# A decay mask added by one VectorE instruction per chunk, and the per-token column moved into the bias of eight ScalarE exponentials

## The chip, the cores and the metric

The kernel runs on one core of one Trainium2 chip. The metric is device time in microseconds of one execution. Five engines matter here: TensorE (PE, with its weight loads shown apart as PEld), VectorE (DVE), ScalarE (ACT), GpSimd (POOL) and SyncE (SP), which issues the DMAs. Each engine works through its own instruction queue in order and waits on semaphores of the others.

## The reference, cut to what matters

The program is one layer of a hybrid backbone, run over 128 context tokens and 1024 noisy tokens with the same weights. Its parts are an adaLN modulation, an input projection, a bidirectional chunked scan (SSD) beside a chunk MLP, an output projection, and a squared-ReLU channel MLP. The change lies in the scan, which works in 9 chunks of 128 tokens with 16 heads in 4 groups, once in each direction:

```
a_cum = jnp.cumsum(dtc * A.reshape(G, hg), axis=2)
xdt = xc * dtc[..., None]
seg = a_cum[:, :, :, None] - a_cum[:, :, None, :]
decay = jnp.exp(jnp.where(mask, seg, -jnp.inf))
cb = jnp.einsum('bcign,bcjgn->bcijg', Cc, Bc)
y_diag = jnp.einsum('bcijgh,bcjghp->bcighp', cb[..., None] * decay, xdt)
```

For each chunk, head and direction there is thus a 128x128 matrix exp(row value of token i - column value of token j), masked to one triangle. The kernel folds ln(dt) of token j into the column value, so that the matrix already carries the factor dt.

## The kernel before, in words

Features lie on partitions, tokens on the free axis, in three slices of 384 tokens. Products in full precision are three passes of rounded high and low parts (`product`, L182). A weight tile is split into these parts by `split` (L167): ScalarE makes the high part, and GpSimd or VectorE makes the low part by a subtraction (L169).

The input projection is a stream of 32 column tiles (L549 to L554): for each of the 4 groups B, C and two x tiles and some u tiles, then eight z tiles. The order of TensorE's work is written out by hand: `product` calls `tick` three times on the way, and `tick` runs a piece of a generator: a convolution pass (`conv`, L607), transposes, or a piece of `scan` (L680). The other engines' queues are ordered by a planner that goes by its own costs and by the order of the program.

`scan(g, G)` first walks the chunks backward to build the states of the backward direction (L742 to L756), then forward over all nine chunks (L760 to L795). Per chunk the forward loop updates the state `Hf` (TensorE into the one bank `Sps`, VectorE L765), builds the matrices of the chunk three further on with `mats` (L710), multiplies into the one bank `yp` (L785), and ScalarE copies that bank out (L788).

`mats(c)` is called 36 times, 9 per group. It loads `ap`, 128 partitions (token j) by 8 x 128 (4 heads of either direction, token i), broadcast from DRAM. For c > 0 ScalarE writes `ea = exp(ap)` (L717) and GpSimd multiplies it by C (L718). Then VectorE runs eight instructions on 128x128 each (L720), which add to `ap` the column value `lcol` of token j as a per-partition scalar and the mask of the direction; ScalarE takes two exponentials of 128x512 (L723); VectorE adds the two directions into `M` (L725), and GpSimd multiplies by C B (L726).

Of the kernel before, what the change touches and what calls it, by code (L numbers as in the profile page):

```python
# [10 lines left out]
AF = mybir.ActivationFunctionType  # L11
# [3 lines left out]
P = 128  # L15
# [15 lines left out]
# columns of the table of per-feature vectors, features on partitions  # L31
# [33 lines left out]
def cut(c0, c1):  # L65
    """Columns c0:c1 by the sequence they belong to: (start, stop, v)."""
    if c0 < TP < c1:
        return [(c0, TP, 0), (TP, c1, 1)]
    return [(c0, c1, int(c0 >= TP))]
# [10 lines left out]
def cc(c):  # L80
    """Columns of chunk c in a convolved tile, which keeps a gap of 4 behind the prompt."""
    return slice(c * P + 4, c * P + 4 + P) if c else slice(0, P)
# [3 lines left out]
def hybrid_layer(ctx, tc, i, y_out, st_out):  # L86
# [14 lines left out]
    def phase(**sizes):  # L101
        # a phase's pools; each tile waits only for the last users of its own bytes
        nonlocal stack
        stack.close()
        stack = ExitStack()
        for nm in list(pools):
            if nm not in ("x1", "sq"):
                del pools[nm]
        for nm, n in sizes.items():
            pools[nm] = stack.enter_context(tc.tile_pool(name=nm, bufs=n, reuse_waits="tile"))  # L110
# [19 lines left out]
    # ---- scratch in DRAM  # L130
# [9 lines left out]
    # ---- constants  # L140
# [30 lines left out]
    def wtile(src, name, tag="w", lo_eng=None):  # L171
        """A weight tile of 1024 words per partition as its high and low part."""
        if tag == "w":
            raw = wp.tile([P, KD, P], F32, tag="raw", name=name + "r", bufs=2)
            hi, lo = (wp.tile([P, KD, P], F32R, tag="w", name=name + x, bufs=4) for x in "hl")
        else:
            raw = tl(tag + "r", name + "r", (KD, P))
            hi, lo = (tl(tag, name + x, (KD, P), F32R) for x in "hl")
        nc.sync.dma_start(raw, src)
        split(hi, lo, raw, lo_eng or nc.gpsimd)  # L180
        return hi, lo

    def product(ps, w, act, beside=None):
        """ps = W.T @ act over the 8 k-tiles, in three passes of rounded parts; beside() runs three times on the way."""
        wh, wl = w
        ah, al = act
        n = 0
        for k in range(KD):
            for a, b in ((wh, ah), (wh, al), (wl, ah)):
                nc.tensor.matmul(ps, a[:, k, :], b[:, k, :], start=n == 0, stop=n == 3 * KD - 1)  # L190
                n += 1
                if beside and n % KD == 0:
                    beside()

    def rms_factor(reds, name):
        """1/sqrt(mean of squares + eps) of the columns, on all partitions; reds: squares that add up over the features."""
        w = reds[0].shape[-1]
        ps = mps(name + "p", w)
        for n, r in enumerate(reds):
            nc.tensor.matmul(ps, ones, r, start=n == 0, stop=n == len(reds) - 1)  # L200
        rs = med(name + "s", (w,))
        nc.scalar.activation(rs, ps, AF.Sqrt, bias=eps_t, scale=1.0 / D)
        nc.vector.reciprocal(rs, rs)
        return rs

    def modulate(xk, s, gain, sh0, hs, rs, ks=range(KD)):
        """h = x * rs * gain + shift for token slice s, as high and low part."""
        c0 = s * SL
        for a, b, v in parts(s):
            r = slice(a - c0, b - c0)  # L210
            for k in ks:
                o = med("hn")[:, :b - a]
                nc.vector.scalar_tensor_tensor(out=o, in0=xk[k][:, r], scalar=gain[:, k, v:v + 1], in1=rs[:, r],
                                               op0=ALU.mult, op1=ALU.mult)
                nc.scalar.activation(hs[0][:, k, r], o, AF.Identity, bias=modT[:, sh0 + k, v:v + 1])
                nc.vector.scalar_tensor_tensor(out=hs[1][:, k, r], in0=o, scalar=modT[:, sh0 + k, v:v + 1],
                                               in1=hs[0][:, k, r].bitcast(F32), op0=ALU.add, op1=ALU.subtract)

    # ======== conditioning, positions, first norm
# [18 lines left out]
    def first_ada(q):  # L238
        """Shift and gain of two feature tiles of the first norm, in steps of two k-tiles."""
# [26 lines left out]
    def ada(r):  # L266
        """A third of the modulation vectors, in steps of one k-tile."""
# [29 lines left out]
    def place(x, k, s, eng):  # L297
        """x = feature tile k of token slice s with its positions."""
# [11 lines left out]
    def square(x, acc):  # L310
        """acc + x * x; acc None starts the sum."""
        sq = med("sq")
        nc.scalar.activation(sq, x, AF.Square)
        if acc is not None:
            nc.vector.tensor_tensor(out=sq, in0=sq, in1=acc, op=ALU.add)
        return sq

    def first_norm(s):
        """The rows of token slice s, feature tile by feature tile, and their rms factor."""
# [44 lines left out]
    # ======== dt and v, tokens on partitions; chunk MLP over tokens  # L364
# [3 lines left out]
    # small pieces of work for the tensor engine, run between parts of the products: generators that yield the  # L368
    # least distance to their next piece
# [25 lines left out]
    def v_products(n, k, js, pss, s):  # L395
        """Adds feature tile k to the products of the token chunks js with a third of the columns of dt and v."""
# [11 lines left out]
    # the first products run feature tile by feature tile beside the vectors that their rows need  # L408
# [53 lines left out]
    def mix(s, vgs):  # L462
        """Layer norm of v and its products with the chunk's mixing weights."""
# [28 lines left out]
    def decay_rates():  # L492
        """Softplus, decays; columns: group, direction, head of the group."""
# [13 lines left out]
        # dt  # L507
        nc.vector.scalar_tensor_tensor(out=t0, in0=A, scalar=0.0, in1=t2, op0=ALU.max, op1=ALU.add)
        # ln dt: the argument of a tiny softplus is its logarithm
# [3 lines left out]
        # dt * A, cumulated from either end  # L513
# [35 lines left out]
    # ---- the products of the input projection: kind, number within the kind, column tile  # L549
# [34 lines left out]
    # the first product of the input projection fills the tensor engine while the last mix is under way  # L584
# [8 lines left out]
    # ======== the rest of the input projection; the scan runs beside it  # L593
    phase(xtm=1, mask=1, st=6, M=3, xw=1, xs=6, hf=2, yo=2, cb=1, H=2, B=2, cv=4, xp=2, m=2)
    # added to the exponents: 0 on and below the diagonal, above it for the other direction
# [6 lines left out]
    # ---- pieces of the scan of a group  # L602
# [4 lines left out]
    def conv(kind, g, m, xp):  # L607
        """Convolution, bias and silu of a tile of channels, one pass at a time; then what the scan needs of it."""
# [23 lines left out]
    def totm(src, put, gap):  # L632
        """Transposes of the chunks of src[128 channels, tokens], four at a time."""
# [46 lines left out]
    def scan(g, G):  # L680
        """The scan of group g; yields after pieces of work on the tensor engine."""
# [5 lines left out]
        # states before the sample's chunks: Hb[c] backward, all kept; forward, rolling  # L687
# [18 lines left out]
        def decay(d, c, a, b):  # L706
            """b = the part of the state behind chunk c of direction d that comes from a, the one before it."""
            nc.gpsimd.tensor_tensor(out=heads(b), in0=heads(a), in1=wcol(atot, c, d), op=ALU.mult)

        def mats(c):  # L710
            """The moving operands of chunk c: decayed C B and, per direction, C times the decay from the chunk's edge."""
# [3 lines left out]
            if c:  # L715
                ea = tl("st", "ea", (8, P))
                nc.scalar.activation(ea, ap, AF.Exp)  # L717
                nc.gpsimd.tensor_tensor(out=ea, in0=ea, in1=G.CT[:, cc(c)].unsqueeze(1).to_broadcast([P, 8, P]), op=ALU.mult)  # L718
            for e in range(8):
                nc.vector.scalar_tensor_tensor(out=ap[:, e, :], in0=ap[:, e, :], scalar=lcol[:, c, 8 * g + e:8 * g + e + 1],  # L720
                                               in1=mask[:, e // 4, :], op0=ALU.add, op1=ALU.add)
            for d in (0, 4):
                nc.scalar.activation(ap[:, d:d + 4, :], ap[:, d:d + 4, :], AF.Exp)  # L723
# [74 lines left out]
    # ---- the products  # L798
# [56 lines left out]
    # ======== output projection onto the residual  # L855
# [45 lines left out]
    # chunk-MLP half of the rows  # L901
# [17 lines left out]
    # scan half, then the second norm of a token slice beside the products of the next  # L919
# [26 lines left out]
    # ======== channel MLP  # L946
# [32 lines left out]
    # feature tiles that get their gain before the rms factor is known  # L979
# [47 lines left out]
    # the last two blocks by token slice  # L1027
# [7 lines left out]
def _positions():  # L1035
    """The 2-D position table: features on rows, first by grid row, then by grid column."""
# [11 lines left out]
def _layout(x):  # L1048
# [5 lines left out]
    def wcols(w, cols):  # L1054
        """[tile, partition, k, column] of a weight matrix of 1024 rows."""
# [3 lines left out]
    def gde(a):  # L1059
        """(direction, head) to (group, direction, head of the group) on the last axis."""  # L1060
# [51 lines left out]
```

## Time and profile before

| quantity | value |
|---|---|
| device time, median of 3 runs | 1842.14 us (1841.31 to 1844.1) |
| profiled execution, from its first to its last instruction (span) | 1835.2 us |
| median of the runs less that span | 6.9 us |
| PE busy | 1721.4 us (94%) |
| PEld busy | 1651.2 us (90%) |
| DVE busy | 1105.3 us (60%) |
| ACT busy | 626.4 us (34%) |
| POOL busy | 670.3 us (37%) |

The profile is of one execution, told by its span; the time of the three runs holds some microseconds around it. Busy time of an engine is the time in which an instruction of its is under way, also where that instruction is held up after its start. A row of idle time names what ended it, inferred from semaphores. The share of busy time over the whole span mixes stages with different limits, so the stretch of the scan (about 170 us to 760 us) is read apart.

### The profile page before, as it was taken

To read this page: it belongs to the slowest core of one execution; us is meant where nothing else is said; L and a number is where in the kernel's file an instruction comes from. 1 tells how busy PE (TensorE), PEld (TensorE's weight loads), DVE (VectorE), ACT (ScalarE), POOL (GpSimd) and SP (SyncE) were. 2 spreads that over 40 slices of the span, in tenths; PEclk is the share of its full clock that TensorE was granted. 3 is DMA by queue.
4 is the path that set the end of the run, shared out by engine and by line. 5 is a ranking of instruction groups with operands and counts; after the bars stand their busy time and mean duration, and the time that the engine had idled before them with its cause. 6 is when DMAs were issued, how large, how long until landed. Compare 5 with 4: busy or idle time off the path is not lost.

```text
span 1835.2 us, 26485 instructions
## 1 busy us (share of the span) xinstructions
PE 1721.4 (94%) x10349; PEld 1651.2 (90%) x10349; DVE 1105.3 (60%) x1803; ACT 626.4 (34%) x1045; POOL 670.3 (37%) x493
## 2 busy tenths in 40 slices
PE   6999997897897898899999999999999999999996
PEld 3888997797797787899999999999999999999996
DVE  5956569969969979767388533333333334334427
ACT  4533344454444443354235311122222211111132
POOL 2300225535426426436455422223333222222244
PEclk9999999899898998999999999999999999999999
DMA  9676332242242254685243111111111111111102
GB/s 346 209 245 213 97 135 91 93 145 91 70 152 78 94 204 148 214 297 173 94 127 104 58 46 36 36 45 47 47 46 47 35 35 47 47 35 46 35 12 104
DMA packets 84925, 193.82 MB, mean 106 GB/s; under 512 B 7584, under 2 KB 47552, under 8 KB 84800
## 3 DMA queue, kind: packets, MB, share of 16 engines
q1 hardware_dynamic: 84800, 192.12, 31.5%
q8 instruction: 82, 1.34, 0.3%
q14 instruction: 43, 0.35, 0.1%
HBM read 157.27 MB, written 34.82 MB: 105 GB/s over the span
## 4 chain that ended last, share of the span: by engine, by line
PE 61%; DVE 17%; issue 5%; POOL 2%; ACT 2%; DMA 2%; SPq 0%; DVEq 0%; ACTq 0%; POOLq 0%
PE fps L190 22%; PE gps L970 20%; PE ips L190 10%; DVE ap L720 7%; PE ops L190 6%; DVE cv L613 2%; PE yp L785 1%; DVE xwl L169 1%; DVE x L988 1%; DMA ld<-yz_d 1%; DVE M L725 1%; DVE yt L842 1%; DVE red L930 1%; PE tmp L638 1%; DVE x L868 1%
## 5 line engine op out<-in xcount | busy, mean ns | idle before, releaser
L868 DVE SCALAR_TENSOR_TENSOR x<-gps,modT,x 128x128 f32<-128x128 f32 (+2 forms) x480 | 232.6, 513 | 122.6 <-PE gps L970 122.6
L961 DVE TENSOR_TENSOR fl<-r,fh 128x384 fp32r<-128x384 f32 x96 | 54.1, 565 | 363.4 <-POOL r L960 363.4
L970 PE MATMUL gps<-fh,w2h 128*128 128x384 f32 (+2 forms) x768 | 257.6, 335 | 1.5 <-DVE x L868 1.5
L970 PE MATMUL gps<-fh,w2l 128*128 128x384 f32 (+2 forms) x768 | 256.9, 334 | 0.0
L970 PE MATMUL gps<-fl,w2h 128*128 128x384 f32 (+2 forms) x768 | 256.8, 334 | 0.0
L169 POOL TENSOR_TENSOR w2l<-w2r,w2h 128x1024 fp32r<-128x1024 f32 x31 | 74.6, 2407 | 324.2 <-ACT w2h L168 324.2
L720 DVE SCALAR_TENSOR_TENSOR ap<-ap,lcol,mask 128x128 f32<-128x128 f32 x288 | 178.7, 676 | 5.3 <-ACT ea L717 2.8
L168 ACT CAST w2h<-w2r 128x1024 fp32r<-128x1024 f32 x32 | 33.6, 1051 | 339.9 <-PE gps L970 314.2
L970 PEld LDWEIGHTS gps<-fh,w2h 128*128 128x128 f32 x768 | 144.2, 188 | 2.9 <-DVE x L868 2.1
L970 PEld LDWEIGHTS gps<-fl,w2h 128*128 128x128 f32 x768 | 144.2, 188 | 0.8 <-issue 0.2
L970 PEld LDWEIGHTS gps<-fh,w2l 128*128 128x128 f32 x768 | 144.2, 188 | 0.6
L960 POOL TENSOR_TENSOR r<-r 128x384 f32<-128x384 f32 x96 | 79.7, 831 | 148.7 <-ACT fh L959 148.7
L613 DVE SCALAR_TENSOR_TENSOR cv<-xp,cw,cv 128x1156 f32<-128x1156 f32 x64 | 103.5, 1617 | 28.2 <-ACT cv L610 27.2
L169 POOL TENSOR_TENSOR wil<-wir,wih 128x1024 fp32r<-128x1024 f32 x25 | 60.1, 2404 | 164.3 <-ACT wih L168 160.1
L169 POOL TENSOR_TENSOR wol<-wor,woh 128x1024 fp32r<-128x1024 f32 x32 | 81.4, 2549 | 66.6 <-ACT woh L168 66.5
L958 ACT ACTIVATE r<-fps 128x384 f32<-128x384 f32 x96 | 46.9, 489 | 171.7 <-PE fps L190 170.7
L169 POOL TENSOR_TENSOR w1l<-w1r,w1h 128x1024 fp32r<-128x1024 f32 x32 | 77.0, 2405 | 66.5 <-ACT w1h L168 66.5
L718 POOL TENSOR_TENSOR ea<-ea,cv 128x1024 f32<-128x1024 f32 x32 | 83.9, 2621 | 21.6 <-ACT ea L717 21.1
L190 PE MATMUL ips<-h1h,wih 128*128 128x384 f32 x256 | 90.4, 353 | 0.0
L190 PE MATMUL ips<-h0h,wil 128*128 128x384 f32 x256 | 90.3, 353 | 0.0
L190 PE MATMUL ips<-h0l,wih 128*128 128x384 f32 x256 | 90.3, 353 | 0.0
L190 PE MATMUL ips<-h0h,wih 128*128 128x384 f32 x256 | 90.2, 352 | 0.0
(292 smaller groups left out, 4826.3 us busy)
## 6 DMA issues: line engine op xcount, KB each, us to landing
wa<-in_w_ada_dram SPq DMA_DIRECT2D x48, 512.0 KB, 5.4
wor<-in_w_out_dram SPq DMA_DIRECT2D x40, 512.0 KB, 3.6
ap<-arow_d SPq DMA_DIRECT2D x36, 512.0 KB, 4.1
wir<-in_w_in_dram SPq DMA_DIRECT2D x32, 512.0 KB, 3.8
w1r<-in_w_ff_dram SPq DMA_DIRECT2D x32, 512.0 KB, 3.5
w2r<-in_w_ff_dram SPq DMA_DIRECT2D x32, 512.0 KB, 3.5
mix_d<-vg SPq DMA_DIRECT2D x9, 512.0 KB, 5.1
mxt<-mix_d SPq DMA_DIRECT2D x8, 576.0 KB, 4.7
```

The source lines that it names most:

```text
L168: nc.scalar.copy(hi, src)
L169: lo_eng.tensor_tensor(out=lo, in0=src, in1=hi.bitcast(F32), op=ALU.subtract)
L190: nc.tensor.matmul(ps, a[:, k, :], b[:, k, :], start=n == 0, stop=n == 3 * KD - 1)
L613: nc.vector.scalar_tensor_tensor(out=acc, in0=xp[:, k:k + 1156], scalar=cw[:, 16 * k + m:16 * k + m + 1], in1=acc, op0=ALU.mult, op1=ALU.add)
L638: nc.tensor.transpose(ps[:, c, :], src[:, cc(c0 + c)], ident)
L718: nc.gpsimd.tensor_tensor(out=ea, in0=ea, in1=G.CT[:, cc(c)].unsqueeze(1).to_broadcast([P, 8, P]), op=ALU.mult)
L720: nc.vector.scalar_tensor_tensor(out=ap[:, e, :], in0=ap[:, e, :], scalar=lcol[:, c, 8 * g + e:8 * g + e + 1], in1=mask[:, e // 4, :], op0 ...
L868: nc.vector.scalar_tensor_tensor(out=x1[m][:, a:b], in0=ps[:, a - cols.start:b - cols.start], scalar=modT[:, g0 + m, v:v + 1], in1=x1[m][: ...
L958: nc.scalar.activation(r, ps, AF.Relu)
L960: nc.gpsimd.tensor_tensor(out=r, in0=r, in1=r, op=ALU.mult)
L961: nc.vector.tensor_tensor(out=fl[:, cs], in0=r, in1=fh[:, cs].bitcast(F32), op=ALU.subtract)
L970: nc.tensor.matmul(ps, a[:, m, :], x[:, cols], start=n == 0, stop=n == n1)
```

## The change

`mats` keeps its load, `ea` and the two products on GpSimd. One VectorE addition of 128x1024 now adds the mask to `ap`, the mask tile being read four times per direction by a broadcast view. The column `lcol` is no longer added by VectorE: it goes as bias into the exponential, and since it differs by head and direction, there are now eight exponentials of 128x128 in place of two of 128x512. Everything else in the diff is removed comments.

```diff
         def mats(c):
...
                 nc.scalar.activation(ea, ap, AF.Exp)
                 nc.gpsimd.tensor_tensor(out=ea, in0=ea, in1=G.CT[:, cc(c)].unsqueeze(1).to_broadcast([P, 8, P]), op=ALU.mult)
+            nc.vector.tensor_tensor(out=ap.rearrange("p (d e) i -> p d e i", d=2), in0=ap.rearrange("p (d e) i -> p d e i", d=2),
+                                    in1=mask.unsqueeze(2).to_broadcast([P, 2, 4, P]), op=ALU.add)
             for e in range(8):
-                nc.vector.scalar_tensor_tensor(out=ap[:, e, :], in0=ap[:, e, :], scalar=lcol[:, c, 8 * g + e:8 * g + e + 1],
-                                               in1=mask[:, e // 4, :], op0=ALU.add, op1=ALU.add)
-            for d in (0, 4):
-                nc.scalar.activation(ap[:, d:d + 4, :], ap[:, d:d + 4, :], AF.Exp)
+                nc.scalar.activation(ap[:, e, :], ap[:, e, :], AF.Exp, bias=lcol[:, c, 8 * g + e:8 * g + e + 1])
             M = tl("M", "M", (4, P))
             nc.vector.tensor_tensor(out=M, in0=ap[:, 0:4], in1=ap[:, 4:8], op=ALU.add)
```

## Rows read from the trace of the kernel before

**Rows 1.** The page's first part: engine, busy us (share of span), instructions.
```profile
PE 1721.4 (94%) x10349; PEld 1651.2 (90%) x10349; DVE 1105.3 (60%) x1803; ACT 626.4 (34%) x1045; POOL 670.3 (37%) x493
```

**Rows 2.** The page's fourth part: shares of the last-ending chain by line.
```profile
PE fps L190 22%; PE gps L970 20%; PE ips L190 10%; DVE ap L720 7%; PE ops L190 6%; DVE cv L613 2%; PE yp L785 1%; DVE xwl L169 1%; DVE x L988 1%; DMA ld<-yz_d 1%; DVE M L725 1%; DVE yt L842 1%; DVE red L930 1%; PE tmp L638 1%; DVE x L868 1%
```

**Rows 3.** Busy us (instructions) by stretch; last PE clock, DMA share, GB/s.
```profile
core 0: us, PE busy (x) PEld busy (x) DVE busy (x) ACT busy (x) POOL busy (x), PEclk, DMA share, GB/s
280.00:360.00 80.00, 64.98 (x433) 59.20 (x433) 79.06 (x108) 32.42 (x56) 46.24 (x34) 0.87 0.23 73
400.00:500.00 100.00, 81.05 (x549) 73.80 (x548) 92.69 (x138) 50.51 (x82) 54.13 (x46) 0.91 0.30 95
540.00:640.00 100.00, 79.61 (x543) 72.44 (x542) 95.80 (x136) 45.81 (x77) 56.51 (x44) 0.91 0.29 95
680.00:760.00 80.00, 63.55 (x430) 58.60 (x430) 77.71 (x124) 31.73 (x59) 48.34 (x33) 0.89 0.43 143
sum 360.00, PE 289.19 PEld 264.05 DVE 345.26 ACT 160.47 POOL 205.21; mean PE 72.30 PEld 66.01 DVE 86.32 ACT 40.12 POOL 51.30
```

**Rows 4.** Waits in 170:760: engine, line, waited for: us, times, longest us.
```profile
ACT ap L723 <- DVE ap L720: 123.6, 52, 7.7
...
PE Sps L704 <- DVE Hf L765: 34.2, 15, 4.6
...
PE Sps L704 <- DVE H L751: 18.4, 12, 2.7
PE yp L785 <- ACT yt L788: 16.8, 11, 4.5
```

**Rows 5.** Timeline of DVE, 471.5 to 479.2: start us, us, instruction, count.
```profile
472.86 5.99 DVE L720 SCALAR_TENSOR_TENSOR ap<-ap,lcol,mask 128x128 f32<-128x128 f32 x5
478.77 0.41 DVE L765 TENSOR_TENSOR Hf<-Hf,Sps 128x256 f32<-128x256 f32 x1
```

**Rows 6.** Timeline of POOL, 471.5 to 479.2.
```profile
472.61 0.80 POOL L708 TENSOR_TENSOR H<-H,atot 128x256 f32<-128x256 f32 x1
473.37 2.46 POOL L718 TENSOR_TENSOR ea<-ea,cv 128x1024 f32<-128x1024 f32 x1
475.79 2.39 POOL L169 TENSOR_TENSOR wil<-wir,wih 128x1024 fp32r<-128x1024 f32 x1
```

**Rows 7.** Tile ap: ns min/median/max of one instruction, first and last start us.
```profile
L720 DVE SCALAR_TENSOR_TENSOR ap<-ap,lcol,mask x288: 334/340/2593, 181.7 to 752.2; 128x128 f32<-128x128 f32 x144
L723 ACT ACTIVATE ap<-ap x72: 614/630/634, 182.9 to 752.5; 128x512 f32<-128x512 f32 x72
L725 DVE TENSOR_TENSOR M<-ap x36: 674/680/2557, 184.9 to 753.2; 128x512 f32<-128x512 f32 x36
```

**Rows 8.** Timelines of DVE: five masks alone; a 128x1024 subtraction and its follower.
```profile
569.95 1.39 DVE L720 SCALAR_TENSOR_TENSOR ap<-ap,lcol,mask 128x128 f32<-128x128 f32 x5
...
714.04 1.21 DVE L169 TENSOR_TENSOR wil<-wir,wih 128x1024 fp32r<-128x1024 f32 x1
715.18 0.54 DVE L841 SCALAR_TENSOR_TENSOR th<-th,ips 128x384 f32<-128x384 f32 x1
```

**Rows 9.** Busy time of L720 alone in the four stretches.
```profile
280.00:360.00 80.00, 43.77 (x60) 0.87 0.23 73
400.00:500.00 100.00, 44.69 (x72) 0.91 0.30 95
540.00:640.00 100.00, 50.32 (x72) 0.91 0.29 95
680.00:760.00 80.00, 26.93 (x61) 0.89 0.43 143
```

**Rows 10.** ACT by line and form: busy us, mean ns | idle before it.
```profile
L215 ACT ACTIVATE h1h<-hn,modT 128x384 fp32r<-128x384 f32 x8 | 4.5, 615 | 1.5 <-DVE hn L213 1.5
...
L215 ACT ACTIVATE h0h<-hn,modT 128x128 fp32r<-128x128 f32 x8 | 2.9, 397 | 7.9 <-DVE hn L213 7.9
```

**Rows 11.** Timeline of ACT: three instructions with a bias from SBUF, and two masks' exponentials.
```profile
68.30 1.68 ACT L215 ACTIVATE h1h<-hn,modT 128x384 fp32r<-128x384 f32 x3 [1.50 <-DVE hn L213]
...
555.38 0.63 ACT L723 ACTIVATE ap<-ap 128x512 f32<-128x512 f32 x1
555.92 1.04 ACT L717 ACTIVATE ea<-ap 128x1024 f32<-128x1024 f32 x1
```

## The prediction

> **What bounds the kernel now.** I read the page first. TensorE is busy 1721.4 of 1835.2 us [rows 1], so over the whole span it looks like the bound and the change, which touches VectorE and ScalarE, like a trifle. But the chain that ended last has one line that isn't TensorE and weighs more than the rest of its kind: the masks on VectorE, L720, with 7% of the span, some 128 us [rows 2]. So the place of the change is on the path, and its stage must be read alone.
>
> I cut the scan into stretches. In four of them (one per group, 360 us together) VectorE is busy 345.26 us and TensorE only 289.19 [rows 3]: here VectorE's queue is hardly ever empty, and TensorE idles 360 - 289.19 = 70.8 us. Its clock is granted at 0.87 to 0.91 in them, so part of the stretch runs at the lower of two levels, 1.2 in place of 2.4 GHz; at 0.87 that part is 0.26 of the stretch, and TensorE fills there time in which it would otherwise wait. The waits say what TensorE stands for: 34.2 us for the state sum L765 and 18.4 us for L751, both short VectorE instructions [rows 4]. They are late because of what is queued ahead of them, and one place shows it: five masks take 5.99 us, and L765 comes right behind [rows 5].
>
> Five masks need not take that long. Where nothing disturbs them five take 1.39 us [rows 8]. Beside the 5.99 us GpSimd runs three instructions back to back, from 472.61 to 478.18 [rows 6]; 5.6 us of these and 5 x 0.26 = 1.3 us of masks make 6.9, less than 1 us over the 5.99. So VectorE and GpSimd take turns there: a mask, which reads two operands in SBUF, stands while a GpSimd instruction is under way. In the four stretches the two engines together are the bound, and that is the reading on which my number rests.
>
> **The change part by part.** *VectorE loses* eight masks per chunk. Undisturbed one lasts 0.34 us [rows 7], and they follow each other every (1.39 - 0.34) / 4 = 0.2625 us [rows 8]; eight hold the engine for 2.10 us. *It gains* one addition of 128x1024 with two operands in SBUF. The trace has the same form as a subtraction of a weight tile: 1.21 us, with the next instruction 1.14 us after its start [rows 8]. The mask's broadcast view isn't in that row, so I bound it: down to 1.14, up to the eight it replaces, 2.10, if the view were read slowly. I take 1.14, since the form and operand type are those of the row. Saved per chunk: 2.10 - 1.14 = 0.96 us.
>
> How many chunks pay? In the four stretches lie 60 + 72 + 72 + 61 = 265 of 288 masks [rows 9], that is 33.1 of 36 chunks; the rest runs where TensorE is the bound and gives nothing. The sum: 33.1 x 0.96 = 31.8 us.
>
> *The time masks were held up* is 43.77 + 44.69 + 50.32 + 26.93 = 165.7 us of busy time [rows 9] less 265 x 0.2625 = 69.6, so 96 us. I cost it at nothing: what GpSimd does is unchanged, and as long as VectorE's queue is never empty, the time that one instruction no longer stands is stood by the next. The other end is that it goes with the instructions, for one start per chunk in place of eight; that is the first rival.
>
> The Trainium skill bears on this choice (SBUF — State Buffer, section "Who interferes with whom"): a VectorE instruction with two SBUF inputs and a GpSimd instruction that reads SBUF exclude each other, and the second to issue stands until the first ends. The trace agrees at the place of [rows 5, 6]. By this rule the turns cost what both engines execute, whatever number of instructions it is cut into, and the sum stays at 31.8 us; by the masks' mean busy time in the four stretches, 165.7 / 265 = 0.63 us each, it would be 33.1 x (8 x 0.63 - 1.21), over 120 us and more than all of TensorE's idle time there.
>
> *ScalarE loses* two exponentials of 128x512 per chunk, 0.63 us each and 0.54 us apart [rows 7, 11]: 1.17 us. *It gains* eight of 128x128 with a bias from SBUF. The trace has that form: 0.397 us [rows 10]. One of 128x384 takes 0.615 us [rows 10] and three together 1.68 [rows 11], so each begins (3 x 0.615 - 1.68) / 2 = 0.08 us before its predecessor's end; an estimate from that is 0.40 + 7 x 0.32 = 2.6 us for eight. ScalarE gets 2.6 - 1.17 = 1.43 us more per chunk, 47 us over 33.1 chunks. In the four stretches it is busy 160.5 of 360 us [rows 3], afterwards about 208, still 58%; and for 123.6 us it stood waiting for masks [rows 4], which come sooner now. That cover hides the 47 us. Without it they lie in front of the copy L788, which frees the one bank `yp`: see the third rival.
>
> *The addition M* (L725) now waits for an exponential that ends about 2.6 us after the mask, not 0.63. Queued behind it on VectorE are state sums for which TensorE waits. What hides this is other VectorE work between mask and M: passes of the convolution, weighing, the next chunk's mask. The matrices are built three chunks ahead of their use, so their own lateness costs nothing. I take nothing for it; bounds: zero, and (2.6 - 0.63) x 33.1 = 65 us.
>
> No DMA, no queue of SP and no instruction of GpSimd is added or moved. What is late next in the four stretches: still GpSimd and VectorE in turn, since TensorE keeps 70.8 - 31.8 = 39 us of idle time there.
>
> **The sum.** The span 1835.2 less 31.8 is 1803.4 us. The median of the runs, 1842.14, is 6.9 us above this span, for what lies around it and from run to run; with that, 1810.3 us. I predict 1810 us, with 1800 to 1823 as this case's own range: its upper end lets a fifth of the bound of M's wait be paid (13 us), its lower end lets a tenth of the 96 us of hold-ups go after all (10 us).
>
> **The rivals.**
> *First: the hold-ups go with the instructions.* One start per chunk meets GpSimd once. Half of the 96 us goes, VectorE's queue runs empty at times, and TensorE's waits for the two state sums vanish: 34.2 + 18.4 = 52.6 us [rows 4], up to the whole 70.8. Time: 1842 - 57 = 1785, from 1771 to 1795. For it: single masks were stretched to 2.59 us [rows 7], and the first of them is released by the same exponential `ea` as GpSimd's product. Against it: VectorE is busy 96% of the four stretches, so something else stands next.
>
> *Second: M's wait eats it.* If M stands right behind the mask in VectorE's queue in half of the chunks, 33 of 65 us come back: 1842 - 32 + 33 = 1843, no change that shows.
>
> *Third, slower: ScalarE is late for TensorE.* In place: the copy L788 out of the only `yp` bank, for which TensorE already waits 16.8 us [rows 4]. If the copy stands behind the eight exponentials, the next chunk's product starts 1.43 us later, 51 us over 36 chunks: 1842 - 32 + 51 = 1861. It decides once more than six tenths of the chunks (31.8 of 51) pay. For it: one bank, one in-order queue. Against it: ScalarE's long waits for the masks, which shrink.
>
> *Fourth: it doesn't do what it says.* The addition with its broadcast mask takes 2.10 us like the eight masks; VectorE wins nothing, ScalarE's 47 us stay hidden: 1842.
>
> **How the numbers follow.** My case 0.48, the first rival 0.27, the second 0.10, the third 0.10, the fourth 0.05. A measurement of this kernel tells a change of about 0.2% (3.7 us) from none. The first two cases are faster by more: 0.75; of the second and fourth rival half, 0.05 to the faster side if they eat a little less than all, which makes 0.80; 0.08 within; 0.12 slower, from the third rival and a little of the second. The range 1775 to 1842 leaves out the lower end of the first rival (0.05) and the slower cases (0.13).
>
> **What would show it right or wrong.** Right: L720 shows 36 additions with a minimum near 1.2 us and some of 2 to 4; VectorE's busy time falls by far more than 32 us only if its queue runs empty; L723 shows 288 exponentials near 0.39 us; TensorE's idle time between 280 and 730 us falls by about 32 us, with its waits for L765 and L751 shrunken; nothing outside the scan changes. Wrong by the first rival: VectorE below 90% busy in these stretches and TensorE's idle time nearly gone. By the second: idle time of VectorE before M, ended by L723. By the third: TensorE's wait for L788 grown from 16.8 us to over 40. By the fourth: the shortest addition at 2 us.

## The result and the profile after

The changed kernel took 1808.22 us (median of 4 runs, 1807.15 to 1808.8) beside 1841.72 us for the kernel before: a ratio of 0.9822, interval 0.9808 to 0.9836, or 33.5 us less. The profiled execution has a span of 1805.4 us, 29.8 less than before; the medians and the spans come from different executions, so the two differences need not agree. All of the 29.8 us comes from the scan: from 170 us to the last copy out of `yp` it takes 565 us in place of 595, and from there to the end both kernels take 1070 us.

The page of the changed kernel begins so; it answers to [rows 1, 2]:

```profile
PE 1711.6 (95%) x10349; PEld 1644.1 (91%) x10349; DVE 1068.3 (59%) x1551; ACT 669.7 (37%) x1261; POOL 704.3 (39%) x493
...
PE fps L190 22%; PE gps L969 21%; PE ops L190 7%; PE ips L190 7%; DVE ap L719 3%; DVE cv L613 2%; ACT ap L722 2%; DVE xwl L169 1%; DVE xw L696 1%; DVE M L724 1%; DVE x L987 1%; PE yp L784 1%; DVE red L929 1%; DVE h20l L216 1%; DVE x L867 0%
```

The masks' line on the last-ending chain has gone from 7% to 3%, and the exponentials have come in with 2%. GpSimd, whose instructions are the same, is busy 34 us longer; the place shown at the end of this section says why. (Line numbers behind `mats` are one lower now.)

The tile `ap` in the changed kernel (ns min/median/max, first and last start), against [rows 7]:

```profile
L722 ACT ACTIVATE ap<-ap,lcol x288: 384/388/415, 183.1 to 724.0; 128x128 f32<-128x128 f32 x144
...
L719 DVE TENSOR_TENSOR ap<-ap,mask x36: 1210/2154/3426, 181.8 to 719.9; 128x1024 f32<-128x1024 f32 x36
L724 DVE TENSOR_TENSOR M<-ap x36: 676/688/2570, 187.3 to 724.4; 128x512 f32<-128x512 f32 x36
```

The addition's shortest instance, 1.21 us, is the row it was taken from [rows 8], so the broadcast view of the mask costs nothing. Its median is 2.15 us: most of the 36 additions are held up. The exponentials take 0.388 us.

The four stretches of the changed kernel (they lie elsewhere now), against [rows 3], and below them the waits from 170 to 740 us, against [rows 4]:

```profile
core 0: us, PE busy (x) PEld busy (x) DVE busy (x) ACT busy (x) POOL busy (x), PEclk, DMA share, GB/s
280.00:360.00 80.00, 66.80 (x486) 61.47 (x485) 76.35 (x61) 49.03 (x115) 54.53 (x33) 0.94 0.26 82
400.00:480.00 80.00, 68.53 (x492) 62.58 (x491) 73.35 (x61) 51.89 (x121) 56.97 (x39) 0.94 0.25 84
520.00:620.00 100.00, 87.31 (x594) 80.92 (x593) 94.39 (x80) 60.28 (x138) 67.19 (x45) 0.91 0.32 104
640.00:730.00 90.00, 74.68 (x511) 69.09 (x511) 81.49 (x89) 48.94 (x121) 60.55 (x38) 0.93 0.51 173
sum 350.00, PE 297.31 PEld 274.06 DVE 325.58 ACT 210.13 POOL 239.24; mean PE 74.33 PEld 68.51 DVE 81.40 ACT 52.53 POOL 59.81
```

```profile
ACT ap L722 <- DVE ap L719: 63.7, 28, 7.8
...
PE Sps L704 <- DVE Hf L764: 17.2, 8, 4.0
...
DVE M L724 <- ACT ap L722: 11.8, 8, 3.9
...
PE Sps L704 <- DVE H L750: 9.7, 10, 1.6
...
PE Sps L704 <- DVE xwl L169: 9.3, 4, 4.7
...
PE yp L784 <- ACT yt L787: 7.2, 6, 2.3
PE yp L784 <- POOL Hf L708: 6.8, 2, 3.8
```

VectorE is still busy 93% of these stretches (325.6 of 350). TensorE's waits for the two state sums are halved, 52.6 to 26.9 us, and its wait for ScalarE's copy fell rather than grew. Part of that comes back elsewhere: its wait for `xwl` on VectorE rose from 2.8 to 9.3 us, and 6.8 us for GpSimd's `Hf` are new.

Where the hold-ups went is the step to see most closely. VectorE's groups in the scan, before (170 to 765 us) and after (170 to 735 us), as busy us, mean ns | idle before:

```profile
L720 DVE SCALAR_TENSOR_TENSOR ap<-ap,lcol,mask 128x128 f32<-128x128 f32 x288 | 178.7, 676 | 5.3 <-ACT ea L717 2.8 <-DMA ap<-arow_d 2.4
L613 DVE SCALAR_TENSOR_TENSOR cv<-xp,cw,cv 128x1156 f32<-128x1156 f32 x64 | 103.5, 1617 | 28.2 <-ACT cv L610 27.2
L169 DVE TENSOR_TENSOR xwl<-xw,xwh 128x256 fp32r<-128x256 f32 x64 | 38.1, 596 | 10.5 <-ACT xwh L168 10.5
L696 DVE TENSOR_TENSOR xw<-xtm,wst 128x256 f32<-128x256 f32 x64 | 35.5, 555 | 1.4 <-ACT xtm L671 0.4
L725 DVE TENSOR_TENSOR M<-ap 128x512 f32<-128x512 f32 x36 | 26.5, 735 | 3.9 <-ACT ap L723 3.9
```

```profile
L613 DVE SCALAR_TENSOR_TENSOR cv<-xp,cw,cv 128x1156 f32<-128x1156 f32 x64 | 109.7, 1714 | 25.3 <-ACT cv L610 24.1
L719 DVE TENSOR_TENSOR ap<-ap,mask 128x1024 f32<-128x1024 f32 x36 | 81.1, 2257 | 6.4 <-ACT ea L717 3.4 <-DMA ap<-arow_d 3.0
L696 DVE TENSOR_TENSOR xw<-xtm,wst 128x256 f32<-128x256 f32 x64 | 57.6, 899 | 1.7 <-ACT xtm L671 0.3
L169 DVE TENSOR_TENSOR xwl<-xw,xwh 128x256 fp32r<-128x256 f32 x64 | 52.2, 816 | 10.5 <-ACT xwh L168 10.1
L724 DVE TENSOR_TENSOR M<-ap 128x512 f32<-128x512 f32 x36 | 31.2, 867 | 11.9 <-ACT ap L722 11.8
```

The masks' line lost 97.6 us of busy time, yet the scan is only 30 us shorter. Of the 178.7 us, 288 x 0.2625 = 75.6 were execution and 103 hold-up; of the 81.1 now, 36 x 1.14 = 41 are execution and 40 hold-up. The 63 us of hold-up that left the masks turn up in lines that the change does not edit: 22.1 in `xw`, 14.1 in `xwl`, 6.2 in `cv`, 4.7 in M, together 47, and the rest in smaller lines. VectorE as a whole is busy 455.8 us in the scan where it was 490.9, 35 us less, and the execution saved is 75.6 - 41.0 = 34.6. One place of the changed kernel shows it, first VectorE, then GpSimd, from 425 to 437 us:

```profile
424.72 1.21 DVE L719 TENSOR_TENSOR ap<-ap,mask 128x1024 f32<-128x1024 f32 x1
425.86 1.51 DVE L169 TENSOR_TENSOR xwl<-xw,xwh 128x256 fp32r<-128x256 f32 x1
427.40 2.50 DVE L696 TENSOR_TENSOR xw<-xtm,wst 128x256 f32<-128x256 f32 x1
```

```profile
424.88 2.21 POOL L725 TENSOR_TENSOR M<-M,cb 128x512 f32<-128x512 f32 x1 [0.63 <-DVE M L724]
427.04 2.57 POOL L718 TENSOR_TENSOR ea<-ea,cv 128x1024 f32<-128x1024 f32 x1
```

The mask runs unhindered, and GpSimd's M, 1.27 us when it is alone, takes 2.21 since it begins beside it. Then `xwl` and `xw`, 0.41 us each when alone, last 1.51 and 2.50 us, standing for GpSimd's two products.

### The profile page after: what moved, and what is told of

Its sections match the earlier page's. It is cut to its first block, busy times and chain, and to the rows that moved or that the text cites. A ratio compares the mean times of both kernels' runs of the same rounds, so it can differ in the third digit from the quotient of the medians.

```text
span 1805.4 us, 26426 instructions
## 1 busy us (share of the span) xinstructions
PE 1711.6 (95%) x10349; PEld 1644.1 (91%) x10349; DVE 1068.3 (59%) x1551; ACT 669.7 (37%) x1261; POOL 704.3 (39%) x493
## 4 chain that ended last, share of the span: by engine, by line
PE 60%; DVE 14%; issue 5%; ACT 4%; POOL 1%; DMA 1%; DVEq 0%; SPq 0%; ACTq 0%; POOLq 0%
PE fps L190 22%; PE gps L969 21%; PE ops L190 7%; PE ips L190 7%; DVE ap L719 3%; DVE cv L613 2%; ACT ap L722 2%; DVE xwl L169 1%; DVE xw L696 1%; DVE M L724 1%; DVE x L987 1%; PE yp L784 1%; DVE red L929 1%; DVE h20l L216 1%; DVE x L867 0%
## 5 line engine op out<-in xcount | busy, mean ns | idle before, releaser
L169 POOL TENSOR_TENSOR wil<-wir,wih 128x1024 fp32r<-128x1024 f32 x25 | 63.7, 2549 | 161.2 <-ACT wih L168 157.3
L613 DVE SCALAR_TENSOR_TENSOR cv<-xp,cw,cv 128x1156 f32<-128x1156 f32 x64 | 109.7, 1714 | 25.3 <-ACT cv L610 24.1
L722 ACT ACTIVATE ap<-ap,lcol 128x128 f32<-128x128 f32 x288 | 89.4, 391 | 63.8 <-DVE ap L719 63.7
L718 POOL TENSOR_TENSOR ea<-ea,cv 128x1024 f32<-128x1024 f32 x32 | 95.2, 2975 | 8.8 <-ACT ea L717 8.8
L190 PE MATMUL ips<-h1h,wil 128*128 128x384 f32 x256 | 88.2, 345 | 0.0
```

The lines of the kernel that those rows point to most:

```text
L169: lo_eng.tensor_tensor(out=lo, in0=src, in1=hi.bitcast(F32), op=ALU.subtract)
L613: nc.vector.scalar_tensor_tensor(out=acc, in0=xp[:, k:k + 1156], scalar=cw[:, 16 * k + m:16 * k + m + 1], in1=acc, op0=ALU.mult, op1=ALU.add)
L722: nc.scalar.activation(ap[:, e, :], ap[:, e, :], AF.Exp, bias=lcol[:, c, 8 * g + e:8 * g + e + 1])
```

## The experiments

The theory under test: VectorE and GpSimd take turns in the scan, so that what both execute sets its time, and ScalarE's extra work is hidden. The rivals: the hold-ups leave with the instructions; VectorE's queue alone is the bound; ScalarE's work counts. Each ratio is against the kernel before on the same chip; the change itself is at 0.982.

**ScalarE's half alone.**

```diff
-            nc.vector.tensor_tensor(out=ap..., in1=mask.unsqueeze(2)..., op=ALU.add)
+            for e in range(8):
+                nc.vector.tensor_tensor(out=ap[:, e, :], in0=ap[:, e, :], in1=mask[:, e // 4, :], op=ALU.add)
```

> ScalarE's half of the change alone: eight exponentials with the column as bias, while VectorE still adds the mask in eight instructions of 128x128. Theory (VectorE and GpSimd take turns, and what the two execute sets the scan's time): VectorE executes 8 x 0.26 = 2.1 us per chunk as before, ScalarE's 47 us more are hidden, so about 1842 us, 1836 to 1848. Rival (ScalarE's work counts): slower than before, up to 1842 + 47 = 1889 us. Rival (the number of VectorE instructions doesn't matter, only that the column is gone): near 1808 us.

Measured: 1830.42 us, 0.9953 (0.9938 to 0.9968): 8.7 us faster than before, where no change was expected. Its rows of `ap` and TensorE's waits say why:

```profile
L720 DVE TENSOR_TENSOR ap<-ap,mask x288: 273/279/2496, 181.9 to 742.5; 128x128 f32<-128x128 f32 x144
```

```profile
PE Sps L704 <- DVE Hf L764: 27.6, 13, 4.2
PE yp L784 <- ACT yt L787: 25.6, 16, 3.6
```

Eight additions in a row, from its VectorE timeline:

```profile
348.38 1.69 DVE L720 TENSOR_TENSOR ap<-ap,mask 128x128 f32<-128x128 f32 x8
```

A mask without the column lasts 0.279 us, not 0.340, and the next begins (1.69 - 0.28) / 7 = 0.20 us after it, not 0.26. Eight cost 8 x 0.061 = 0.49 us less, 16 us over 33.1 chunks. Against that, TensorE's wait for ScalarE's copy is 25.6 us in place of 16.8: the third rival's mechanism is there, at 9 us (for 21.8 of the 25.6 us the copy stood right behind the masks' exponentials in ScalarE's queue). 16 less 9 is near the 8.7 measured; that the two make it up is worked out, not shown by itself.

**The same with a constant in place of the column.** This asks which part of the old form cost the 0.06 us.

```diff
-            nc.vector.tensor_tensor(out=ap..., in1=mask.unsqueeze(2)..., op=ALU.add)
+            for e in range(8):
+                nc.vector.scalar_tensor_tensor(out=ap[:, e, :], in0=ap[:, e, :], scalar=0.0, in1=mask[:, e // 4, :], op0=ALU.add, op1=ALU.add)
```

> Eight masks of 128x128 on VectorE in the form of before, but with the constant 0 in place of the column from SBUF, and eight exponentials with the column as bias. Eight plain additions took 0.279 us each where the form with the column took 0.340, and that kernel was at 0.995 of before. If the scalar from SBUF is what costs 0.06 us, these last 0.28 us and the time is about 0.995 of before, 1833 us; if the form with two operations costs it, 0.34 us and 1.000 of before or a little over.

Measured: 1831.35 us, 0.9954 (0.9935 to 0.9973), and the median of one is 0.278 us:

```profile
L720 DVE SCALAR_TENSOR_TENSOR ap<-ap,mask x288: 274/278/2499, 184.2 to 746.4; 128x128 f32<-128x128 f32 x144
```

The order in every engine's queue is the same in this kernel and in that of ScalarE's half alone. So it is the scalar read from SBUF, not the second operation.

**VectorE's half alone.**

```diff
-            for e in range(8):
-                nc.scalar.activation(ap[:, e, :], ap[:, e, :], AF.Exp, bias=lcol[...])
+            for d in (0, 4):
+                nc.scalar.activation(ap[:, d:d + 4, :], ap[:, d:d + 4, :], AF.Exp)
```

> VectorE's half of the change alone: one mask addition of 128x1024, and two exponentials of 128x512 without bias, so the per-token column is left out of the matrices. Theory: the same gain as the whole change, 1804 to 1811 us, since ScalarE's 47 us were hidden. Rival (ScalarE's eight exponentials cost part of the gain): 1775 to 1800 us.

Measured: 1817.55 us, 0.9884 (0.9869 to 0.9898): 21.5 us faster than before, but 12 short of the change, though ScalarE is busy 264 us in the scan and not 307. Neither side expected that. TensorE's order of work is the same; the order in the queues of VectorE, ScalarE and GpSimd differs, since the planner orders them anew. The wait for L764 is 30.2 us here and 17.2 in the change.

**Eight exponentials without the column** was to tell the number of exponentials from the column's absence.

```diff
-                nc.scalar.activation(ap[:, e, :], ap[:, e, :], AF.Exp, bias=lcol[...])
+                nc.scalar.activation(ap[:, e, :], ap[:, e, :], AF.Exp)
```

> One mask addition of 128x1024 and eight exponentials of 128x128 without a bias, so the per-token column is left out of the matrices. With two exponentials of 128x512 and no column the time was 0.988 of before, 12 us over the changed kernel, although ScalarE had less to do. If the number of exponentials (and the order of the queues that comes with it) makes this difference, 0.982, about 1808 us; if the column's absence does, 0.988, about 1820 us.

Measured: 1812.67 us, 0.9854 (0.9836 to 0.9873), halfway between the two answers: inconclusive. One exponential without the bias takes 0.294 us:

```profile
L722 ACT ACTIVATE ap<-ap x288: 292/294/327, 182.3 to 720.6; 128x128 f32<-128x128 f32 x144
```

Why a kernel with less ScalarE work comes out 6 to 12 us later stays open; another order of the queues is the likely cause, argued and not shown.

This bears on the change itself, for its queues are in another order than before too. VectorE runs 122 other instructions between the masks of a chunk and its M, in place of 66, and M stands right behind the mask in none of the 36 chunks, where it did in three. No run has the change in the order of before, so the order's share of the 33.5 us is not known. The three kernels with the same mask addition and three orders gain 21.5, 26.7 and 33.5 us: some 21 us come with any of them, and up to 12 may be the order's.

**No mask at all.**

```diff
-            nc.vector.tensor_tensor(out=ap..., in1=mask.unsqueeze(2)..., op=ALU.add)
             for e in range(8):
-                nc.scalar.activation(ap[:, e, :], ap[:, e, :], AF.Exp, bias=lcol[...])
+                nc.scalar.activation(ap[:, e, :], ap[:, e, :], AF.Exp, bias=eps_t)
```

> The mask addition is left out altogether, and the eight exponentials take a constant column as bias, so ScalarE works as in the changed kernel. Theory: another 33 x 1.14 = 38 us of VectorE's execution leaves the turns: about 1770 us, 1765 to 1785 (TensorE is idle for 58 us of the scan, so there is room). Rival (after the change TensorE's own order or another wait is the bound): 1800 to 1808 us.

Measured: 1774.5 us, 0.965 (0.9636 to 0.9664): 64.6 us below before, 31 below the change, where 38 were expected. Taking away execution still pays after the change (here too the queues' order differs).

**The mask on GpSimd.**

```diff
-            nc.vector.tensor_tensor(out=ap..., in1=mask.unsqueeze(2)..., op=ALU.add)
+            nc.gpsimd.tensor_tensor(out=ap..., in1=mask.unsqueeze(2)..., op=ALU.add)
```

> The mask addition of 128x1024 moved from VectorE to GpSimd. Theory (turns): GpSimd takes about 2.4 us for a product of this size where VectorE takes 1.14 us, so the two execute 33 x 1.25 = 41 us more: about 1849 us, 1835 to 1865. Rival (VectorE's queue alone is the bound, GpSimd has time to spare at 39% busy): VectorE is rid of 81 us of busy time, so faster than the change, 1770 to 1800 us.

Measured: 1865.69 us, 1.0142 (1.0125 to 1.0159): slower than before by 26.6 us and than the change by 60. VectorE was freed (434.6 us busy in the scan, not 455.8) and the kernel lost, so its queue alone was not the bound. The loss passes the 41 us of the theory; the groups of GpSimd and the waits show what was left out:

```profile
L719 POOL TENSOR_TENSOR ap<-ap,mask 128x1024 f32<-128x1024 f32 x36 | 100.9, 2803 | 0.7 <-DMA ap<-arow_d 0.7
```

```profile
ACT ap L722 <- POOL ap L719: 119.1, 32, 8.8
PE yp L784 <- ACT yt L787: 54.6, 22, 5.8
```

ScalarE stands 119 us for the masks, nearly twice as long as in the change (63.7), and behind it the copy out of `yp` is late: TensorE waits 54.6 us for it, and for 39.1 of these the copy stood right behind the masks' exponentials. The wait is the third rival's, but here it comes from the late masks, not from longer work on ScalarE.

**GpSimd's products moved to VectorE.** `ea` times C, M times C B, both, and both with the low parts of the weights:

```diff
-                nc.gpsimd.tensor_tensor(out=ea, in0=ea, in1=G.CT..., op=ALU.mult)
+                nc.vector.tensor_tensor(out=ea, in0=ea, in1=G.CT..., op=ALU.mult)
...
-            nc.gpsimd.tensor_tensor(out=M, in0=M, in1=G.cb..., op=ALU.mult)
+            nc.vector.tensor_tensor(out=M, in0=M, in1=G.cb..., op=ALU.mult)
...
-            wn = wtile(i["w_in"]..., "wi", lo_eng=nc.vector if kind in LO_DVE else nc.gpsimd)
+            wn = wtile(i["w_in"]..., "wi", lo_eng=nc.vector)
```

> On top of the change, the product of ea with C (128x1024, 32 times) moved from GpSimd to VectorE. Theory (turns): 2.35 us of GpSimd become 1.14 us of VectorE in some 30 chunks of the four stretches, 30 x 1.2 = 36 us less of both together: about 1772 us, 1765 to 1790, since TensorE's 58 us of idle time leave room. Rival (VectorE's queue is the bound): 30 x 1.14 = 34 us slower, about 1842 us.

> On top of the change, the product of M with C B (128x512, 36 times) moved from GpSimd to VectorE. Theory (turns): 1.27 us of GpSimd become 0.60 us of VectorE, 33 x 0.67 = 22 us less: about 1786 us, 1780 to 1797. Rival (VectorE's queue): 33 x 0.6 = 20 us slower, about 1828 us.

> Both products, ea with C and M with C B, moved from GpSimd to VectorE on top of the change. Theory (turns): 36 + 22 = 58 us less of both together, as much as TensorE's idle time in the scan; with some of that left, 1755 to 1780 us. Rival (VectorE's queue): 54 us slower, about 1862 us.

> As with both products moved, and the low parts of the input projection's weights (128x1024, 25 subtractions) also moved from GpSimd to VectorE. Theory (turns): 2.4 us of GpSimd become 1.14 us of VectorE some 15 times in the stretches, 19 us less of both; by then TensorE is nearly the bound, so 1750 to 1775 us. Rival (VectorE's queue): slower than with both products alone by 15 x 1.14 = 17 us.

| moved to VectorE | us | ratio (interval) | less than before |
|---|---|---|---|
| `ea` times C | 1779.08 | 0.9673 (0.9658 to 0.9687) | 60.1 us |
| M times C B | 1799.67 | 0.9788 (0.9773 to 0.9803) | 39.5 us |
| both | 1772.9 | 0.9644 (0.9628 to 0.966) | 66.3 us |
| both and the low parts | 1750.45 | 0.9518 (0.9504 to 0.9533) | 88.8 us |

Each gives VectorE more to do, and each is faster than the change (33.5 us): VectorE's queue as the only bound is refuted. The sizes are less sure than the direction. Beyond the change, `ea` gave 27 us where 36 were expected, M 6 where 22 were, both 33 where 58 were, and the low parts another 22 where 19 were: the sum of both engines' execution is not always what is gained. With all three moved, the rows of the mask and the waits of TensorE read:

```profile
L719 DVE TENSOR_TENSOR ap<-ap,mask x36: 1206/1212/1695, 181.4 to 661.6; 128x1024 f32<-128x1024 f32 x36
```

```profile
PE Sps L704 <- DVE xwl L169: 9.3, 8, 1.9
PE Sps L704 <- DVE Hf L764: 2.8, 2, 1.4
```

The median mask falls from 2.15 to 1.21 us with no edit to it: what it had stood for was GpSimd. The scan, 170 us to the last copy, takes 507 us, of which TensorE is busy 488.

**The kernel before with the same moves.** This is the sharpest test of the first rival: with GpSimd out of the way there are hardly any hold-ups to remove.

> The kernel before (eight masks with the column, two exponentials), but with the products of ea and M and the low parts of the weights moved from GpSimd to VectorE, so that nearly nothing takes turns with VectorE. Against the changed kernel with the same moves (0.952 of before) this prices the change where GpSimd is out of the way. Theory (turns): VectorE alone is busy some 410 + 36 of about 520 us and TensorE is nearly the bound, so the change is worth less than its 32 us here: this kernel at 0.957 to 0.963 of before, 1762 to 1773 us. Rival (the hold-ups of single masks were what the change removed): without GpSimd there are none, so the same as with the change, 0.950 to 0.954.

```profile
L720 DVE SCALAR_TENSOR_TENSOR ap<-ap,lcol,mask x288: 333/340/1099, 182.1 to 692.8; 128x128 f32<-128x128 f32 x144
```

Measured: 1778.37 us, 0.9665 (0.9649 to 0.968). The longest mask is 1.1 us, not 2.6, all masks together are busy 89.5 us in the scan, some 14 over their execution of 75.6, and still the change is worth 88.8 - 61.0 = 27.8 us there. So the gain does not need the hold-ups; the execution saved, 34.6 us, is the cause that is left beside the order of the queues. TensorE's longest wait in this kernel is for ScalarE's high parts:

```profile
PE Sps L704 <- ACT xwh L168: 16.4, 7, 4.0
```

It is 1.0 us with the change and the same moves. ScalarE makes `xwh` from VectorE's `xw`, and each of the seven began within 0.8 us of the end of its `xw`, so this too is a wait for VectorE. The change pays more than I expected of a scan so near TensorE's bound (0.957 to 0.963).

**All of GpSimd's products and sums in the scan and the z tiles moved.** On top of the three moves above:

```diff
-            nc.gpsimd.tensor_tensor(out=heads(b), in0=heads(a), in1=wcol(atot, c, d), op=ALU.mult)
+            nc.vector.tensor_tensor(out=heads(b), in0=heads(a), in1=wcol(atot, c, d), op=ALU.mult)
...
-                    nc.gpsimd.tensor_tensor(out=sqa[:, cs], in0=sqa[:, cs], in1=sq, op=ALU.add)
+                    nc.vector.tensor_tensor(out=sqa[:, cs], in0=sqa[:, cs], in1=sq, op=ALU.add)
```

> The changed kernel with every product and sum of the scan and of the z tiles moved from GpSimd to VectorE: ea, M, the low parts of the weights, the decayed states and the sum of squares. Theory (turns): 67 states and sums of 0.6 to 1.1 us of GpSimd become 0.33 to 0.47 us of VectorE, about 25 us less of both, but TensorE has only 19 us of idle time left there and most of it is not a wait for VectorE: 1743 to 1750 us, 0.947 to 0.952 of before. Rival (VectorE's own queue is now the bound): slower than 1755 us.

Measured: 1749.15 us, 0.9504 (0.9487 to 0.9521), within the interval of the kernel with three moves: nothing more to win there. Both beat the change by some 57 us.

## Why the prediction was right

*The bound.* Right: the scan gave all of it, and the moves and the mask on GpSimd show that VectorE and GpSimd together were the limit. How much a microsecond of execution is worth there is shown less well, since the moves gave from a quarter of the expected gain to a little more than all of it.

*VectorE's saving, 31.8 us.* Right in its sum, and the measured 33.5 us (29.8 in the spans) lie near it. That they lie so near is partly luck: kernels with the same mask addition and no more work on ScalarE gained 21.5 and 26.7 us, and the sum held no term for the order of the queues. ("No instruction of GpSimd is added or moved" is true of the program text; in the traces GpSimd's order differs too.) The 6.9 us from the span to the median was 2.8 us in the changed kernel, which made up for the 2 us by which the span came out longer than expected. Also, the 0.96 us per chunk hide two savings that I took for one: 0.49 us since the masks no longer read a scalar from SBUF (2.10 to 8 x 0.20 = 1.61), and 0.47 us since eight instructions became one (1.61 to 1.14).

*The hold-ups at nothing.* Right, and shown twice: they moved to `xw`, `xwl`, `cv` and to GpSimd (busy 263 to 296 us in the scan), and with GpSimd out of the way the change kept 27.8 of its 33.5 us. (The first rival's 57 us follow from no row; its two waits add up to 52.6, which would have made it 1789 us.) The Trainium skill's rule (SBUF — State Buffer, section "Who interferes with whom") gave the same sum; the rows agree, the place at 425 to 437 us above all.

*ScalarE hidden.* Right for the change (TensorE's wait for its copy 16.8 to 7.2 us), wrong as a rule: 9 us of it showed where VectorE's masks stayed eight. The exponentials cost 0.388 us, 0.397 expected, and ScalarE is busy 43 us more over all 36 chunks, where 1.43 us per chunk would make 51.

*M's wait at nothing.* Nearly: VectorE's idle time before M rose from 3.9 to 11.8 us, 8 of the bound of 65. What hides the rest is other VectorE work between mask and M, as the prediction said; but there is nearly twice as much of it as before, by the new order, which the prediction did not foresee.

*TensorE's idle time down by 32 us.* Wrong in kind. The scan of both kernels, with the columns of [rows 3]:

```profile
170.00:765.00 595.00, 517.02 (x3368) 484.35 (x3368) 490.92 (x708) 263.64 (x451) 262.53 (x211) 0.94 0.37 121
```

```profile
170.00:735.00 565.00, 506.74 (x3362) 476.48 (x3362) 455.76 (x454) 307.36 (x666) 295.87 (x211) 0.95 0.39 127
```

The idle time fell by 20, from 595 - 517.0 = 78.0 to 565 - 506.7 = 58.3 us (from 66.9 to 54.5 between 280 and 730 us, the window that the prediction named). The other 10 us are TensorE's busy time for the same work, at a granted clock of 0.95 in place of 0.94. The prediction had read the lower clock as filling time that was lost anyway; a third of the gain lies in that busy time.

## What to carry to other kernels

Before pricing an edit on VectorE, see whether its instructions last longer than their minimum and what GpSimd does meanwhile: where GpSimd is what holds them up, as here, the hold-up passes to the next VectorE instruction as long as VectorE's queue is full, so count the execution that is saved and not the busy time that disappears. Where the two take turns, a product that GpSimd does in 2.4 us and VectorE in 1.2 can be better on VectorE even if that engine is the busier one: here it gained 27 us. Where a planner orders the queues, an edit of one line can move other lines too; leave some 10 us for that in a kernel like this one. And price the scalar operand of an instruction by itself: on a 128x128 tile it was nearly a fifth of the time (0.061 of 0.340 us).

## What the runs showed of the hardware

A scalar read from SBUF costs VectorE 0.06 us per instruction on 128x128 (0.340 against 0.278 us with a constant, same operation). A bias read from SBUF costs ScalarE 0.094 us (0.388 against 0.294 us for an exponential of 128x128 without one). A mask tile read through a broadcast view cost nothing beside a plain operand (1.21 us both, on 128x1024). A VectorE instruction with two operands in SBUF stood while a GpSimd product or subtraction was under way: the median mask fell from 2.15 to 1.21 us when GpSimd's work was moved away.
